# The first two feed-forward blocks of a streaming encoder layer, quarter by quarter while the rows are being turned

## The chip, the cores and the metric

One Trainium2 chip, one of its cores. The kernel is one launch on that core: one layer of a streaming encoder. The metric is the device time of one execution in microseconds (us), lower is better. The kernel before has a median of 2502.78 us over 3 runs (2499.66 to 2502.88).

Engines are named as in the profile: PE is the matrix engine (PEld its weight loads), DVE the vector engine, ACT the scalar engine, POOL the general engine, SP the engine that issues most transfers. Each engine works through its own instructions in the order in which they stand in the built program; an instruction that waits holds up all behind it on its engine.

## The reference, cut to what matters

The layer is a feed-forward block, a mixer (attention and a recurrent branch, merged by gates) and a second feed-forward block, on T = 1072 frames (16 meta tokens, 1024 prompt frames, 32 frames of running streams) of D = 1024 channels.

```python
D_MODEL = 1024
SEQ = 1024
DEC_SEQ = 32
N_META = 16
D_FF = 2816
EPS = 1e-6

def rmsnorm(x, g):
    xf = x.astype(jnp.float32)
    y = xf * lax.rsqrt(jnp.mean(xf * xf, axis=-1, keepdims=True) + EPS)
    return (y * g.astype(jnp.float32)).astype(x.dtype)

def half_ffn(x, g, w_gate, w_up, w_down):
    h = rmsnorm(x, g)
    return x + 0.5 * ((jax.nn.silu(h @ w_gate) * (h @ w_up)) @ w_down)
...
def reference(...):
    ...
    x = half_ffn(x, ffn1_norm[l], ffn1_w_gate[l], ffn1_w_up[l], ffn1_w_down[l])
    h = rmsnorm(x, mix_norm[l])
    ... (mixer)
    x = half_ffn(x, ffn2_norm[l], ffn2_w_gate[l], ffn2_w_up[l], ffn2_w_down[l])
    ... (final norm)
```

The change is at the start of the first feed-forward (the norm and the first columns of `h @ w_gate`, `h @ w_up`) and at the same place of the second.

## The kernel before, in words

**Products in three parts.** Each float32 operand is split in a high part (`xh`, `whi`; a copy that rounds, on ACT) and a low part (`xl`, `wlo`; the difference, on DVE). A product is `whi*xh + whi*xl + wlo*xh`. `product()` makes one such product for four 128-row slices of the channels (half of the 1024, called `kh` 0 or 1) and one quarter of the frames (268 columns): 12 matmuls of 128x268 into one PSUM bank, all on line L103 of the profile. The split of a tile is `split()` (L219 on ACT, L220 on DVE), that of a weight tile `weights()` (L202 on ACT, L203 on DVE).

**Quarters.** The frames are cut into four quarters of 268, called q0 to q3; `b` is q // 2 and `th` is q % 2. `B[kh, th, b]` is the split pair of half the channels of a quarter.

**The first feed-forward** (`Seven`, tiles of pool `f1`). The 2816 columns are 22 blocks of 128. Blocks 0 and 1 are multiplied plainly by `plain(c)`: for each quarter gate with kh 0 and 1, then up with kh 0 and 1, so 192 matmuls a block and 384 for the two. Blocks 2 to 21 go in pairs ("units", `rest()`) by a scheme of seven half products for two by two; it needs sums of the halves, `T1` to `T4` for each b, made by `sums(b)` (L819, L826, L828, L829, each a 128x1072 DVE operation, and four splits). The gated results are split into a stage (tiles `R`, `st`) and sent to DRAM (`mid_dram`) by POOL.

**What comes before block 0.** The frames are loaded as rows: for each quarter two tiles `xt` of 128 rows, and one tile `odds` that holds the last 12 rows of all four quarters. The row tiles of q0 and q1 lie in slots with the tag `g`, those of q2 in `raw2`, those of q3 in the two slots with the tag `S`. For each quarter `scales` makes the reciprocal root mean square per row (squares summed on ACT, L761; seven small operations on DVE and POOL, L764 to L770, of which POOL's power is L766), `spread` puts it on a diagonal (POOL, L778 and L781), multiplies ones by it on PE and copies the result to `R` (ACT, L783): the scale of each frame in all partitions. `columns(q)` turns the rows: for each of 8 channel slices three PE transposes (two row tiles and the odd rows, all on L106; below, one channel slice of a quarter is called a column), an ACT copy of the turned rows to a tile `s` (L809, sent to DRAM as the residual), a DVE operation that multiplies them by gain and scale (L810), and after each four slices the split into `xh`, `xl`.

**What sets the order.** The tile scheduler that builds the program orders each engine by its own estimates of readiness, unless `PE.on` is set: then PE's instructions keep the order in which they are written. In the first feed-forward it is off before the change. A tile is taken from a tag with so many slots; the first instruction that writes a new tile in a slot waits until the last reader of the tile that was there is done.

**The second feed-forward** begins with `ff.plain(0, ...)`, in written order, behind `out_block`, the last product of the mixer. There the norm of the last 288 frames is still under way while q0 is multiplied: `finish_one()` holds what is left of it (`scale_rows`, L264 and L119 on ACT with the functions Ln and Exp, L267 to L270 on DVE, then `kept`'s multiplications L1661 and splits). `silu` is L119 as well, with another table of functions on ACT; a change of table is an ACT_TABLE_LOAD (L113).

## Time and profile before

| What | Time or share |
|---|---|
| Median of 3 runs (lowest to highest) | 2502.78 us (2499.66 to 2502.88) |
| The profiled execution | 2499.49 us, its span 2497.4 us |
| PE busy in the span | 2403.0 us, 96% |
| DVE, ACT, POOL busy in the span | 67%, 41%, 10% |
| First product of block 0 | 36.70 us |
| First product of unit 1, after blocks 0 and 1 | 97.17 us |
| First product of the second feed-forward | 1764.56 us |

The times in the rows of the profile are us from the start of the span. A row of the timeline is: start, duration, engine, line, operation, written tile, read tiles, shapes, how many in a row, and in square brackets the idle time of the engine just before it with what ended it. In the chain of waits a row is: start, length, engine, tile and line. Durations of neighbours overlap on all engines (a matmul of 268 columns is shown with 0.28 us and the next begins 0.12 us after it), so sums go by starts, or by the chain of waits, which has only what is not covered.

### The profile page before, as it was taken

The numbers are of one execution on the slowest core, as the hardware profiler recorded it, in microseconds if no ns is written. First come the engines' busy times: TensorE is split into PE (matmuls) and PEld (weight loads), VectorE is DVE, ScalarE is ACT, GpSimd is POOL, SyncE is SP. The second block draws the span as 40 slices with busy tenths as digits, with TensorE's granted clock in tenths as the row PEclk, the third lists the DMA queues.
The fourth block names the chain that finished last, engine by engine and source line by source line (L and its number), as shares of the span: only waits on it lengthen the run. The fifth ranks groups of instructions, "written<-read, shape, count | busy, mean of one in ns | idle before, by whom it ended". The sixth has DMA issues, their size and how long they took to land.

```text
span 2497.4 us, 47900 instructions
## 1 busy us (share of the span) xinstructions
PE 2403.0 (96%) x19500; PEld 2299.1 (92%) x19500; DVE 1669.2 (67%) x3144; ACT 1021.3 (41%) x2129; POOL 257.2 (10%) x461
## 2 busy tenths in 40 slices
PE   6999999989998999999999999999799999989997
PEld 5999999979998999999788888999799999989997
DVE  4767676758865377774666665556966767666876
ACT  6444444542225243332545544323544444443223
POOL 1001010100003011221000000111011111110000
PEclk9999999999999999999999999999899999999999
DMA  7334343477651211111211122522244444467761
GB/s 197 105 122 166 122 166 122 164 292 280 245 210 62 60 44 56 48 49 53 57 44 49 44 64 67 190 86 98 75 136 153 143 147 147 143 266 267 274 235 71
DMA packets 270371, 331.93 MB, mean 133 GB/s; under 512 B 41078, under 2 KB 228726, under 8 KB 264518
## 3 DMA queue, kind: packets, MB, share of 16 engines
q1 hardware_dynamic: 247942, 244.96, 29.7%
q0 software_dynamic: 22208, 83.91, 8.9%
q8 instruction: 153, 2.51, 0.4%
q14 instruction: 68, 0.56, 0.1%
HBM read 213.93 MB, written 114.89 MB: 132 GB/s over the span
## 4 chain that ended last, share of the span: by engine, by line
PE 54%; issue 29%; DVE 6%; DMA 4%; POOL 4%; ACT 3%; POOLq 0%; SPq 0%; DVEq 0%; ACTq 0%
PE ps_mm L103 20%; PE ps_z L103 11%; PE pu L103 6%; PE ps_o L103 5%; PE pv L103 4%; PE pf L103 4%; POOL mid_dram L353 3%; DMA mid_dram<-st 2%; PE ps_tr L103 2%; PE ps_tr L106 2%; PE ps_z L106 1%; DMA u_xl<-mid_dram 1%; DVE wlo L203 1%; PE ps_mm L106 0%; DVE acc L1661 0%
## 5 line engine op out<-in xcount | busy, mean ns | idle before, releaser
L103 PE MATMUL ps_mm<-xh,whi 128*128 128x384 f32 (+2 forms) x952 | 316.8, 333 | 0.5 <-DVE raw L1455 0.5
L103 PE MATMUL ps_mm<-xh,wlo 128*128 128x384 f32 (+2 forms) x952 | 310.4, 326 | 0.0
L103 PE MATMUL ps_mm<-xl,whi 128*128 128x384 f32 (+2 forms) x952 | 309.9, 326 | 0.0
L219 ACT ACTIVATE whi<-S 128x1024 fp32r<-128x1024 f32 x122 | 129.2, 1059 | 310.7 <-PE ps_z L103 138.0
L353 POOL DMA_DIRECT2D mid_dram<-st x148 | 102.7, 702 | 872.7 <-DVE st L220 854.9
L103 PEld LDWEIGHTS ps_mm<-xh,whi 128*128 128x128 f32 x952 | 179.3, 188 | 9.0 <-issue 5.0
L103 PEld LDWEIGHTS ps_mm<-xl,whi 128*128 128x128 f32 x952 | 179.4, 188 | 1.1
L103 PEld LDWEIGHTS ps_mm<-xh,wlo 128*128 128x128 f32 x952 | 179.5, 189 | 0.3
L220 DVE TENSOR_TENSOR wlo<-S,whi 128x1024 fp32r<-128x1024 f32 x122 | 149.2, 1223 | 37.8 <-ACT whi L219 35.2
L220 DVE TENSOR_TENSOR st<-g,st 128x536 fp32r<-128x536 f32 (+1 forms) x148 | 103.5, 709 | 100.2 <-ACT st L219 100.1
L1247 DVE TENSOR_TENSOR_SCAN left<-left,oneb 128x512 f32<-128x512 f32 (+6 forms) x112 | 107.4, 959 | 54.8 <-ACT left L119 54.2
L202 ACT ACTIVATE whi<-raw 128x1024 fp32r<-128x1024 f32 x67 | 70.5, 1056 | 172.6 <-PE ps_mm L103 135.8
L219 ACT ACTIVATE st<-g 128x536 fp32r<-128x536 f32 (+1 forms) x148 | 93.5, 643 | 96.6 <-DMA mid_dram<-st 82.4
L220 DVE TENSOR_TENSOR wlo<-raw,whi 128x1024 fp32r<-128x1024 f32 x80 | 76.6, 958 | 72.6 <-ACT whi L219 70.9
L103 PE MATMUL ps_z<-acc1s,whi 128*128 128x268 f32 (+1 forms) x480 | 106.3, 285 | 0.0
L103 PE MATMUL ps_z<-xh1s,whi 128*128 128x268 f32 (+1 forms) x360 | 102.8, 286 | 0.0
L103 PE MATMUL ps_z<-xl1s,whi 128*128 128x268 f32 (+1 forms) x360 | 102.6, 285 | 0.0
L103 PE MATMUL ps_z<-xh1s,wlo 128*128 128x268 f32 (+1 forms) x360 | 102.6, 285 | 0.0
L103 PE MATMUL ps_z<-xh2s,whi 128*128 128x268 f32 (+1 forms) x352 | 100.5, 286 | 2.2 <-ACT s L458 2.2
L103 PE MATMUL ps_z<-xl2s,whi 128*128 128x268 f32 (+1 forms) x352 | 100.4, 285 | 0.0
L103 PE MATMUL ps_z<-xh2s,wlo 128*128 128x268 f32 (+1 forms) x352 | 100.3, 285 | 0.0
L203 DVE TENSOR_TENSOR wlo<-raw,whi 128x1024 fp32r<-128x1024 f32 x67 | 82.8, 1240 | 23.3 <-ACT whi L202 23.1
(719 smaller groups left out, 7636.2 us busy)
## 6 DMA issues: line engine op xcount, KB each, us to landing
mid_dram<-st POOLq DMA_DIRECT2D x74, 536.0 KB, 4.2
mid_dram<-st POOLq DMA_DIRECT2D x74, 528.0 KB, 3.9
raw<-in_ffn_w_gate_dram SPq DMA_DIRECT2D x44, 512.0 KB, 3.8
raw<-in_ffn_w_up_dram SPq DMA_DIRECT2D x44, 512.0 KB, 3.9
raw<-in_w_in_dram SPq DMA_DIRECT2D x44, 512.0 KB, 3.7
raw<-in_ffn_w_down_dram SPq DMA_DIRECT2D x40, 512.0 KB, 5.3
u_xl<-mid_dram SPq DMA_DIRECT2D x8, 1608.0 KB, 6.5
u_xh<-mid_dram SPq DMA_DIRECT2D x8, 1608.0 KB, 10.4
```

Source lines behind the costliest of these rows:

```text
L103: return self.queue(nc.tensor.matmul(*args, **more))
L106: return self.queue(nc.tensor.transpose(*args, **more))
L202: A.activation(hi, raw, AF.Copy)
L203: V.tensor_tensor(lo, raw, hi.bitcast(F32), op=ALU.subtract)
L219: A.activation(dst_h, src, AF.Copy)
L220: V.tensor_tensor(dst_l, src, dst_h.bitcast(F32), op=ALU.subtract)
L353: nc.gpsimd.dma_start(self.mids[i, :, :, NAMES.index(name)], st.bitcast(F32))
L1247: V.tensor_tensor_scan(rev(st[:rows]), rev(st[:rows]), one, 1.0 if carry is None else carry[:rows], op0=ALU.mult, op1=ALU.mult)
```

## The change

- `plain` takes several blocks. Blocks 0 and 1 of the first feed-forward are multiplied together: for each quarter, kh 0 of gate 0, up 0, gate 1, up 1 (steps j = 0 to 3), then kh 1 of the same (j = 4 to 7); 12 matmuls a step. PE's order is as written (`PE.on`). Behind single steps other work is emitted: after j = 0 of q1, q2, q3 the columns of that quarter's kh 1; after j = 3 `spread` of the next quarter, and the scales and the diagonal of the quarter after it (now on POOL); after j = 5 the columns of the next quarter's kh 0; `sums(0)` after j = 6 of q2, `sums(1)` after j = 1 of q3.
- The loads on SP stand in another order: rows of q0, odd rows, gate and up weights of block 0, rows of q1 and q2, then the weights of block 1 among the rows of q3. The four weight tiles use the two slots of `raw`.
- q0 is turned by a function of its own (`first_columns`): rows of the first row tile first, diagonal on DVE, splits in halves of two channel slices (128x536), the eighth slice behind the second step.
- One Square of 1024 elements in place of two of 512. `odds` is cleared on DVE in place of POOL.
- `sums` makes all four differences first, then the splits; T1, T2, T3 get other homes, T4 of b = 0 is split at once.
- Products of a tile of zeros (128x512, bf16) are put on PE: 18 at the start, 6 ahead of the first ones-by-diagonal, 5 ahead of the first product.
- In the second feed-forward q0 of block 0 now goes gate kh 0, up kh 0, gate kh 1, up kh 1, with both weights requested ahead, and `finish_one()` is called after the silu of the quarter.
- Two small operations (`causalb`, `lmax`) are tied behind a product, so that they don't come early.

The diff, without the parts that only pass results on:

```diff
-        def plain(self, c, before=lambda q: None, after=lambda q: None):
+        def plain(self, cs, step=lambda q, j: None, tags=(None,) * 2):
...
             for q in range(4):
-                before(q)
                 b, th = divmod(q, 2)
-                pss = []
-                for wh, wl in (gw, uw):
-                    ps = bank(rotate=True)
-                    for kh in range(2):
-                        ks = slice(kh * 512, (kh + 1) * 512)
-                        product(ps, (wh[:, ks], wl[:, ks]), self.B[kh, th, b], kh == 0)
-                    pss.append(ps)
-                after(q)
-                silu(where(g, th, b), pss[0][:, :qw])
-                V.tensor_tensor(where(g, th, b), pss[1][:, :qw], where(g, th, b), op=ALU.mult)
+                pss = [bank(tag, tag is None) for tag in tags]
+                for kh in range(2):
+                    ks = slice(kh * 512, (kh + 1) * 512)
+                    for j, (wh, wl) in enumerate(x for c in cs for x in ws[c]):
+                        product(pss[j], (wh[:, ks], wl[:, ks]), self.B[kh, th, b], kh == 0)
+                        to = where(gs[cs[j // 2]], th, b)
+                        if kh and j % 2 == 0:
+                            silu(to, pss[j][:, :qw])
+                        elif kh:
+                            V.tensor_tensor(to, pss[j][:, :qw], to, op=ALU.mult)
+                        step(q, kh * len(pss) + j)
...
+        row_tiles(0)
+        for x in range(4):
+            load(odds, 32 * x, x * QW + 2 * P, ODD)
+        raw_weights(0)
+        row_tiles(1)
+        row_tiles(2)
+        raw_weights(1)
+        row_tiles(3)
...
+        def warm(n, ps):
+            for _ in range(n):
+                PE.matmul(ps, busy[:, :P], busy[:, P:P + 512], start=True, stop=True)
...
         def sums(b):
 
             v11, v12, v21, v22 = (value(*x, b) for x in ((0, 0), (0, 1), (1, 0), (1, 1)))
-            t1, t2 = f32s("S"), f32s("S")
+            t1, t2, t4, t3 = f32s("S"), f32s("S"), f32s("s"), f32s("s")
             V.tensor_tensor(t1, v12, v11, op=ALU.subtract)
...
             V.tensor_tensor(t2, v22, t1, op=ALU.subtract)
+            V.tensor_tensor(t4, v21, t2, op=ALU.subtract)
             V.tensor_tensor(t3, v22, v12, op=ALU.subtract)
...
+        def step(q, j):
+            if (q, j) == (0, 1):
+                first_rest()
+            if q < 3:
+                if j == 3:
+                    spread(q + 1)
+                    if q < 2:
+                        diagonal(q + 2, scales(rows[2 * q + 4:2 * q + 6], G, latest[0]), odd, G)
+                elif j == 5:
+                    columns(q + 1, 0)
+            if q and j == 0:
+                columns(q, 1)
+            if (q, j) in ((2, 6), (3, 1)):
+                sums(q - 2)
+
+        ff.plain((0, 1), step, ("mm", "mm", "tr", "o"))
...
-        ff.plain(0, after=lambda q: finish_one())
+        ff.ahead[0] = [gate0[0], ff.block(ffn2_w_up, 0)]
+        ff.plain((0,), lambda q, j: j == 3 and finish_one())
```

Three places where the order of instructions moves:

DVE around the turning of q3. `S` and `s` are the tiles of `sums`, `xl2s` is the low part of q3, `acc0s`, `acc1s` and `xe` hold the scaled frames. Before:

```order
L810 SCALAR_TENSOR_TENSOR acc1s<-ps_z,gains,R 128x268
L819 TENSOR_TENSOR S<-acc0s 128x1072
L220 TENSOR_TENSOR xl2s<-acc1s,xh2s 128x1072
L826 TENSOR_TENSOR S<-acc0s,S 128x1072
L390 TENSOR_TENSOR g<-ps_z,g 128x268
L220 TENSOR_TENSOR acc2s<-S,acc2s 128x1072
L829 TENSOR_TENSOR s<-xe_126,S 128x1072
L828 TENSOR_TENSOR S<-acc0s 128x1072
```

And in the change (L846 is the old L810, L229 the old L220, L903 to L906 are the differences of `sums`):

```order
L846 SCALAR_TENSOR_TENSOR acc1s<-ps_z,gains,R 128x268 x4
L229 TENSOR_TENSOR xl2s<-acc1s,xh2s 128x1072
L397 TENSOR_TENSOR g<-ps_o,g 128x268
L903 TENSOR_TENSOR S<-acc0s 128x1072
L904 TENSOR_TENSOR S<-acc0s,S 128x1072
L905 TENSOR_TENSOR s<-xe_137,S 128x1072
L906 TENSOR_TENSOR s<-acc0s 128x1072
L229 TENSOR_TENSOR xe_768<-S,xe_767 128x1072
L229 TENSOR_TENSOR xl1s<-s,xh1s 128x1072
L229 TENSOR_TENSOR acc0s<-S,acc0s 128x1072
L229 TENSOR_TENSOR xe_769<-s,acc0s 128x1072
```

Directly behind these eight stand `L846 ... acc1s` x4, the last four channel slices of q3, then L903 of `sums(1)` and the last `xl2s`. So the four differences and four splits of `sums(0)` stood behind the last scaling of q3, and now stand ahead of its second half.

ACT at the second feed-forward: `ms` and `ys` are the norm of the last 288 frames, `g` the silu of a quarter. Before:

```order
L264 ACTIVATE ms<-ps_z,epsb 128x288
L119 ACTIVATE ys<-ms 128x288
L119 ACTIVATE ys<-ys 128x288
L113 ACT_TABLE_LOAD
L119 ACTIVATE g<-ps_z 128x264
L119 ACTIVATE g<-ps_tr 128x264
L219 ACTIVATE acc0s<-S 128x1056
L219 ACTIVATE xh1s<-acc_17872 128x4x24 x2
```

And in the change:

```order
L119 ACTIVATE g<-ps_z 128x264
L273 ACTIVATE ms<-ps_z,epsb 128x288
L119 ACT_TABLE_LOAD
L119 ACTIVATE ys<-ms 128x288
L228 ACTIVATE acc0s<-S 128x1056
L119 ACT_TABLE_LOAD
L119 ACTIVATE ys<-ys 128x288
L119 ACT_TABLE_LOAD
L119 ACTIVATE g<-ps_mm 128x264
L228 ACTIVATE xh1s<-acc_17873 128x4x24 x2
```

The silu of q0 went ahead of Ln and Exp (the two `ys`), and a table load stands ahead of each of Ln, Exp and the next silu; the table of silu itself is loaded some rows earlier (L113). A split (`acc0s`) stands between Ln and Exp.

SP at the start. Before:

```order
L734 DMA odds<-in_x_sample_dram 12x1024
L734 DMA xt<-in_x_prompt_dram 128x1024 x5
L734 DMA xt<-in_x_prompt_dram 108x1024
L734 DMA xt<-in_x_sample_dram 20x1024
L192 DMA raw<-in_ffn_w_gate_dram 128x8x128
L192 DMA raw<-in_ffn_w_up_dram 128x8x128
```

And in the change:

```order
L742 DMA odds<-in_x_sample_dram 12x1024
L762 DMA raw<-in_ffn_w_gate_dram 128x8x128
L762 DMA raw<-in_ffn_w_up_dram 128x8x128
L742 DMA xt<-in_x_prompt_dram 128x1024 x4
L762 DMA raw<-in_ffn_w_gate_dram 128x8x128
L742 DMA xt<-in_x_prompt_dram 128x1024
L762 DMA raw<-in_ffn_w_up_dram 128x8x128
L742 DMA xt<-in_x_prompt_dram 108x1024
```

The weights of block 0 passed six row tiles; those of block 1, which stood behind all rows and behind two transfers of the residual, stand among the rows.

More of the change, by code (lines that the diff above doesn't have):

```diff
@@ L183, in tile_encoder_step, with planned, weights @@
     big = Wide
-    def weights(parts, own=None):
-        raw = wp.tile([P, D], F32, tag="raw", name="raw", bufs=2)
+    def planned(made, last):
+        tc.add_manual_dep(made.ins, last.ins.name, order, reason="order")
+    def weights(parts, own=None, raw=None, behind=None, later=None):
         n = 0
+        if raw is None:
+            raw = wp.tile([P, D], F32, tag="raw", name="raw", bufs=2)
         for src, k in parts:
@@ L201, in weights @@
             hi, lo = own()
-        A.activation(hi, raw, AF.Copy)
-        V.tensor_tensor(lo, raw, hi.bitcast(F32), op=ALU.subtract)
+        made = A.activation(hi, raw, AF.Copy)
+        if behind is not None:
+            planned(made, behind)
+        made = V.tensor_tensor(lo, raw, hi.bitcast(F32), op=ALU.subtract)
+        if later is not None:
+            planned(made, later)
         return hi, lo
@@ L838, in sums @@
-            split(*X["T2", b], t2)
-            split(*X["T3", b], t3)
-            return t4
-        def columns_ahead(q):
-            if q == 0:
-                r = scales(rows[0:2] + [odds])
-                found.append(r[2])
-                spread(0, r[:2], found[0])
-                columns(0)
-            if q < 3:
-                spread(q + 1, scales(rows[2 * q + 2:2 * q + 4]), found[0])
-                columns(q + 1)
-        found = []
-        ff.plain(0, columns_ahead)
-        t4s = [sums(b) for b in range(2)]
@@ L855, in tile_encoder_step @@
-        ff.plain(1)
+                X["T1", b] = extra(2, F32R), extra(0, F32R)
+                X["T2", b] = free[:, 0], free[:, 1]
+                X["T3", b] = free[:, 2], extra(3, F32R)
+            else:
+                X["T1", b] = free[:, 0], free[:, 1]
+                X["T2", b] = free[:, 2], extra(1, F32R)
+            split(*X["T1", b], t1)
+            split(*X["T2", b], t2)
+            if b == 1:
+                free = slots("acc", 2, F32R)
+                X["T3", b] = free[:, 0], free[:, 1]
@@ new lines, in sums @@
+            split(*X["T3", b], t3)
+            X["T4", b] = B[0, 1, b]
+            X["B11", b], X["B21", b], X["B22", b] = B[0, 0, b], B[1, 0, b], B[1, 1, b]
+            if b == 0:
+                split(*X["T4", b], t4)
+            else:
+                ff.t4 = t4
+        PE.on = True
+        r = scales([rows[0], odds, rows[1]], V)
+        odd = r[1]
+        wsq = [weights([], None, raws[0][0], latest[0], diagonal(0, [r[0], r[2]], odd, V))]
+        first_rest = first_columns()
+        diagonal(1, scales(rows[2:4], G, latest[0]), odd, G)
@@ new lines, in tile_encoder_step @@
+        up1 = slots("acc", 2, F32R)
+        own = lambda: [up1[:, x].rearrange("p k t -> p (k t)")[:, :D] for x in range(2)]
+        ff.ahead.update({0: wsq, 1: [weights([], own if x else None, raw, latest[0])
+                                     for x, raw in enumerate(raws[1])]})
+        def step(q, j):
+            if (q, j) == (0, 1):
+                first_rest()
+            if q < 3:
+                if j == 3:
[8 more added lines that the diff above has]
+                sums(q - 2)
@@ L856, in tile_encoder_step @@
+        ff.plain((0, 1), step, ("mm", "mm", "tr", "o"))
+        PE.on, PE.last = False, None
+        split(*X["T4", 1], ff.t4)
         constants()
-        for b in range(2):
-            X["T4", b] = B[0, 1, b]
-            split(*X["T4", b], t4s[b])
-            X["B11", b], X["B21", b], X["B22", b] = B[0, 0, b], B[1, 0, b], B[1, 1, b]
         ff.rest()
```

165 lines of the change are left out of this document (102 added, 63 removed).

## The prediction

> **What bounds the kernel now.** I first read the page's shares (PE 96% busy), then a table of windows, since the change touches only the first 120 us and some 30 us at 1764. Its columns: from, to, length; busy time of PE, PEld, DVE, ACT, POOL; granted PE clock; DMA share; GB/s.
>
> ```profile
> 0.00:36.70 36.70, 15.96 (x60) 10.65 (x61) 13.18 (x46) 24.42 (x60) 9.79 (x19) 1.00 0.63 183
> 36.70:64.50 27.80, 27.80 (x180) 24.44 (x181) 18.93 (x35) 14.00 (x26) 1.51 (x3) 1.00 0.88 220
> 64.50:97.20 32.70, 32.70 (x267) 32.70 (x266) 27.78 (x31) 13.72 (x18) 1.42 (x2) 1.00 0.20 66
> 112.00:122.00 10.00, 7.79 (x49) 7.42 (x48) 5.50 (x9) 4.78 (x10) 1.38 (x2) 0.83 0.56 187
> ```
>
> Up to 36.70 PE has no product and is idle for more than half of the time; from there to 97.2, through blocks 0 and 1, it never waits. So two things count: when the first product starts, and whether PE is still fed without a gap. DVE is busy for 46.7 of those 60.5 us, the engine nearest to its limit. PE's waits in the head:
>
> ```profile
> PE ps_z L106 <- DMA xt<-in_x_prompt_dram: 8.2, 2, 7.0
> PE ps_mm L103 <- POOL t_ys L778: 5.7, 1, 5.7
> PE ps_z L103 <- POOL t_ys L778: 3.8, 1, 3.8
> PE ps_mm L103 <- DVE acc0s L810: 2.8, 1, 2.8
> ```
>
> The chain of waits gives prices (start, length, what):
>
> ```profile
> 36.70 5.72 PE ps_mm L103 x24
> 42.42 3.05 PE ps_z L103 x24
> 45.48 0.76 PE ps_tr L103 x6
> 46.24 0.53 PE ps_z L106 x3
> ...
> 70.13 1.19 DVE s L829
> 71.32 1.19 DVE S L828
> 72.54 1.11 ACT acc0s L219
> ...
> 74.13 1.18 DVE acc0s L220
> ```
>
> Twenty-four products take 3.05 us at full clock (0.124 each after rounding over the stretch) and 5.72 at half; one spread 0.76, one column 0.53; a 1072-wide difference or split costs DVE 1.18, and ACT 1.1.
>
> **The change part by part.**
>
> *An earlier first product.*
>
> ```profile
> 9.79 0.63 ACT L761 ACTIVATE t_ms<-xt 128x512 bf16<-128x512 f32 x1 [1.39 <-DMA xt<-in_x_prompt_dram]
> 14.75 0.16 DVE L764 TENSOR_TENSOR ss<-ss 128x3 f32<-128x3 f32 x1 [11.36 <-ACT t_ms L761]
> 16.80 0.16 DVE L770 TENSOR_TENSOR ss<-ss 128x3 f32<-128x3 f32 x1
> 17.74 1.92 PE L103 MATMUL ps_mm<-t_ys,cst 128*128 128x128 f32 x6 [5.70 <-POOL t_ys L778]
> 20.94 0.50 DVE L810 SCALAR_TENSOR_TENSOR acc0s<-ps_mm,gains,R 128x268 f32<-128x268 f32 x1 [0.33 <-ACT s L809]
> 21.36 0.49 DVE L810 SCALAR_TENSOR_TENSOR acc0s<-ps_z,gains,R 128x268 f32<-128x268 f32 x1
> ```
>
> The second row tile lands at 9.79. In the change its square is the last of three: 1.2 us (under two halves of 0.63) gives 11.0. The small chain now takes 14.75 to 16.96 = 2.2; less the addition, 2.0: 13.0. The diagonal on DVE has no row; its three instructions lie between the small operations' 0.16 and the 0.50 of a 268-wide row, 0.5 to 1.5 in all; I take 0.7, nearest to the small rows as 128 elements are few: 13.7. Ones by diagonal 0.76 to 1.92, the copy to R 0.4, two scalings of 0.41 (20.94 to 21.36), half a split 0.55: first product at 17 (16 to 19.5), a **gain of 19.7 us** at that point. The zeros run while PE waits for rows and squares, so 0; the last five can cost up to 1.1, if they stand in the way at half clock.
>
> *PE's work behind it.* Now 16 of 32 columns and two spreads lie before 36.70. In the change only seven columns and one spread do: nine columns (4.8) and one spread (0.76) move into the fed stretch. It then holds 384 products (47.6), 25 columns (13.2), three spreads (2.3): **63.2 us** at full clock. The first 24 products or so are at half clock as now: +2.7 (0 if the zeros had raised it for good).
>
> *Weights.*
>
> ```profile
> L192 SPq DMA_DIRECT2D raw<-in_ffn_w_gate_dram x2: 373/386/400, 11.4 to 35.1; - x2
> DMA to landing us min/median/max: 4.1/7.1/10.4
> 33.88 2.36 DVE L203 TENSOR_TENSOR wlo<-raw,whi 128x1024 fp32r<-128x1024 f32 x2
> ```
>
> Block 0's weights pass six row tiles and are there in time. Block 1's cannot be requested before `raw` is free: gate 1 behind gate 0's `wlo` (about 15.3, right after the diagonal), up 1 behind up 0's (about 20, behind four scalings and two splits). Behind the waiting request on SP stand the rows of q3, which nobody needs before 75. Landing 4.1 to 10.4 later, split in 2.2: gate 1 is ready at 21.6 to 28, up 1 at 26 to 32. PE wants them at about 21 and 24. I take **6 us** of gaps in q0 (3 to 10).
>
> *Each turn to a new quarter.* The next quarter's kh 0 columns end with j = 5; PE then has j = 6 and 7 as cover, 3.0 us. ACT's split stands behind the silu that waits for j = 6 (1.5 us after the columns), then 0.4 for the silu, 1.1 for the high part, 1.2 for the low: 4.2. Gap 1.2, three times: **3.6**.
>
> *The second half of q3, where I expect the loss.* `sums(0)` is emitted before the last columns, and its first two results are written in the two slots `S`, which hold q3's rows: DVE's first difference waits until PE has turned the last column. Only then: four differences, four splits (8 x 1.18 = 9.4), four scalings (1.6), the high split on ACT (1.1), the low one on DVE (1.2): 13.3 us. Behind the waiting difference are queued the scalings that PE's next step needs. PE's cover is j = 1 to 3, 4.5 us. **Gap 8.9**. Were the slots free, DVE could begin about 3.2 us earlier; 5.7 would stay. In the order of before the same 9.4 us lay behind the last scaling, with PE busy on products (64.50 to 97.20 above).
>
> What a gap costs beside itself:
>
> ```profile
> 116.11 0.39 PE L103 MATMUL ps_z<-xh2s,whi 128*128 128x268 f32 x1 [2.17 <-ACT s L458]
> 117.78 0.43 PE L103 MATMUL ps_tr<-xh1s,whi 128*128 128x268 f32 x1
> 121.09 0.29 PE L103 MATMUL ps_z<-xh2s,whi 128*128 128x268 f32 x1
> ```
>
> After a gap of 2.17 us the products ran at half clock from 117.58 to 120.9 (spacing 0.22), 1.5 us lost. A gap of 8.9 costs this too: **+1.7**, at most 3.
>
> Sum for unit 1's first product: 17 + 63.2 + 2.7 + 6 + 3.6 + 8.9 + 1.7 = 103.1, against 97.17: **+5.9** (bounds 94 and 110).
>
> *Unit 1.* The gap of 2.17 and its half clock, 3.7 us, came from ACT waiting on stages that were still being sent. With blocks 0 and 1 ending together and ACT idle in q3, the stages go out elsewhere; but `sums(1)` and unit 1's weight sums now follow right behind the gap and can be late themselves. **-2** (-3.7 to +1.5).
>
> *The second feed-forward.*
>
> ```profile
> 1764.56 0.28 PE L103 MATMUL ps_z<-xh0s,whi 128*128 128x264 f32 x1
> 1774.97 0.59 PE L103 MATMUL ps_mm<-xh0s,wlo 128*128 128x264 f32 x1 [7.11 <-DVE wlo L203]
> 1779.94 1.13 PE L103 MATMUL ps_z<-t_ga,cst 128*128 128x288 f32 x4
> 1781.11 0.50 ACT L264 ACTIVATE ms<-ps_z,epsb 128x288 f32<-128x288 f32 x1 [2.17 <-PE ps_z L103]
> 1782.12 0.44 ACT L119 ACTIVATE ys<-ys 128x288 f32<-128x288 f32 x1
> 1782.59 1.28 ACT L113 ACT_TABLE_LOAD   x1
> 1782.60 0.46 DVE L267 TENSOR_TENSOR ms<-ms,ys 128x288 f32<-128x288 f32 x1
> 1783.88 0.39 ACT L119 ACTIVATE g<-ps_z 128x264 f32<-128x264 f32 x1
> 1785.54 0.45 DVE L270 TENSOR_TENSOR R<-ys,ms 128x288 f32<-128x288 f32 x1
> 1785.65 1.09 ACT L219 ACTIVATE acc0s<-S 128x1056 fp32r<-128x1056 f32 x1 [1.10 <-DVE S L1680]
> 1787.58 0.28 PE L103 MATMUL ps_o<-xl1s,whi 128*128 128x264 f32 x1
> 1787.87 0.26 DVE L220 TENSOR_TENSOR xl1s<-acc,xh1s 128x96 fp32r<-128x96 f32 x1
> ```
>
> PE waits 7.11 us for up's low part, with all 24 gate products done under earlier work. In the new order gate's kh 1 stands behind up's kh 0, which waits for the same `wlo`: 12 products (1.46) come out from under it, and everything behind is 1.46 later. The norm of the last 288 frames gets two table loads (2 x 1.28) and a split (1.09) into its chain, 3.65. DVE's four operations behind Exp took 3.4 us (1782.60 to 1785.99), some 1.4 of it for other work in between that will now be done earlier; q2's operand, which today is there 0.3 us around PE's arrival, is then late by 2.2 to 3.6, less some 15 products of block 1 that the order puts ahead of q2 (1.8): 0.4 to 1.8. **+2.5** (+1 to +5). [...]
>
> Sum: 5.9 - 2 + 2.5 = +6.4. The profiled execution took 2499.49 (2.1 outside its span), so 2505.9; it is the fastest of the runs shown, 3.3 under the median, and I carry the difference to the median: 2509.2, rounded to **2509**.
>
> **The rivals.**
>
> *Not slower (0.13).* One mechanism: the feed of q0. If the weights of block 1 land within 4 us of being requested, and the clock is full from the first product (the zeros count), the 8.7 us of gaps and half clock in q0 go: unit 1 starts at 94.4 (-2.8), and the total is -2.3: 2500. For: 4.1 us is the shortest landing shown. Against: the longest is 10.4, and rows are in transfer at that time. It decides when gate 1's `whi` is ready before 21.
>
> *The gap of q3 is not there (0.13).* If the scalings of q3 were not held (`sums(0)` served before the last columns), unit 1 starts at 92.5, -4.7; the total is -4.2: 2498.6. For: DVE is only busy 85% of 64.50 to 97.20. Against: the slots `S` and the order of DVE.
>
> *No change to speak of (0.16).* The gap is there, PE's head gains as planned, feed gaps of 3, half clock short: unit 1 at 98 to 100, unit 1's own gap gone, +0 to +2: about 2504.
>
> *Worse (0.13).* Block 1's weights land 10 us after the request and half clock stays through q0 (another 24 to 48 products at 0.1 more): unit 1 at 109, total +13: 2516.
>
> The forecast itself has 0.45, 2508 to 2513. A measurement of this kernel can tell about 0.2% (5 us) from no change; below 2497.8 is faster, above 2507.8 slower. Faster 0.12 (half of the second rival, some of the first), same 0.30, slower 0.58. The range 2498 to 2517 leaves out the best of the rivals of the other sign and the tail of the worst.
>
> **What would show it.** Right: first product at 16 to 20; gaps of some us on PE between 20 and 32 with block 1's `whi`, `wlo` or `acc2s` as releasers; one wait of 7 to 9 us on ACT's `xh2s` between 85 and 98, with L903 to L906 and four L229 on DVE under it and the granted clock under 1 behind it; unit 1 at 100 to 106; two more table loads and a PE wait near 9 us at 1766 to 1775. Wrong: a first product after 22; no wait on `xh2s`, or one under 3; unit 1 before 95.

## The result, and the profile after

| | Before | Changed |
|---|---|---|
| Median (lowest to highest), 4 runs each | 2502.83 us (2499.66 to 2505.11) | 2517.80 us (2513.11 to 2520.83) |
| Ratio of the medians, 95% interval | | 1.0060 [1.0047, 1.0073] |
| The profiled execution and its span | 2499.49, 2497.4 | 2520.83, 2518.8 |

The change makes the kernel 15.0 us slower (11.8 to 18.3 by the interval). The forecast was slower by 6.4, 2509, with a range that ended at 2517: the sign was right, the size was not, and the median lies 0.8 us beyond the range.

The windows of the changed kernel's head, with the columns of the prediction's table:

```profile
17.00:36.70 19.70, 17.11 (x88) 14.01 (x88) 9.04 (x16) 11.71 (x22) 5.07 (x11) 0.75 0.77 186
...
84.00:92.00 8.00, 4.35 (x36) 4.13 (x34) 7.88 (x7) 5.20 (x8) 0.00 (x0) 0.99 0.01 2
92.00:103.00 11.00, 6.11 (x29) 5.80 (x30) 9.88 (x13) 4.85 (x8) 0.74 (x1) 0.54 0.27 100
103.00:122.00 19.00, 18.07 (x145) 17.64 (x144) 18.94 (x27) 11.04 (x20) 1.37 (x2) 1.00 0.34 114
```

PE works in q0 (first row) with few gaps but a quarter of the clock missing. From 84 to 103 it works for just over half of the time, while DVE is never idle for long; and it is DVE that stays full, 18.94 of 19.00 us, when PE is busy again. PE's waits in the same kernel up to 170 us (what PE was to do, who ended the wait, us, times, longest):

```profile
PE ps_mm L103 <- ACT xh2s L228: 7.8, 1, 7.8
...
PE ps_mm L103 <- DVE xl1s L229: 1.8, 2, 0.9
PE ps_mm L103 <- DVE xl2s L229: 1.6, 2, 0.9
...
PE ps_tr L103 <- DVE wlo L210: 0.7, 1, 0.7
...
```

The waits for rows and diagonals of 7 and 5.7 us are gone, and one of 7.8 us stands in their place. The timeline of PE in the changed kernel, at its first product, at that wait, and at the first product of unit 1:

```profile
17.08 2.32 PE L103 MATMUL ps_mm<-busy 128*128 128x512 bf16 x5 [1.02 <-DVE acc0s L846]
18.83 0.78 PE L103 MATMUL ps_mm<-xh0s,whi 128*128 128x268 f32 x1
...
88.06 0.28 PE L103 MATMUL ps_o<-xh2s,acc2s 128*128 128x268 f32 x1
96.17 0.59 PE L103 MATMUL ps_mm<-xh2s,whi 128*128 128x268 f32 x1 [7.83 <-ACT xh2s L228]
97.48 0.59 PE L103 MATMUL ps_mm<-xl2s,whi 128*128 128x268 f32 x1 [0.72 <-DVE xl2s L229]
...
105.41 0.29 PE L103 MATMUL ps_mm<-xh0s,whi 128*128 128x268 f32 x1
```

And what DVE does meanwhile:

```profile
83.49 1.27 DVE L903 TENSOR_TENSOR S<-acc0s 128x1072 f32<-128x1072 f32 x1 [3.06 <-PE ps_z L106]
84.86 1.28 DVE L904 TENSOR_TENSOR S<-acc0s,S 128x1072 f32<-128x1072 f32 x1
...
92.10 1.27 DVE L229 TENSOR_TENSOR xe<-s,acc0s 128x1072 fp32r<-128x1072 f32 x1
93.29 1.70 DVE L846 SCALAR_TENSOR_TENSOR acc1s<-ps_z,gains,R 128x268 f32<-128x268 f32 x4
94.91 1.26 DVE L903 TENSOR_TENSOR S<-acc1s 128x1072 f32<-128x1072 f32 x1
96.15 1.27 DVE L229 TENSOR_TENSOR xl2s<-acc1s,xh2s 128x1072 fp32r<-128x1072 f32 x1
```

DVE waits 3.06 us until PE has turned q3's last column (the slots `S`), then does the eight operations of `sums(0)`, and only at 93.29 the four scalings that PE waits for, though PE had turned the first of their columns at 82.1. Unit 1's first product is at 105.41, 8.2 us later than in the kernel before.

That leaves 7 us to find. I numbered PE's matrix instructions, zeros left out, and compared the times at which both kernels reach the same number. The difference grows at four places, two of which lie where no line of the change is: in the mixer, and in a stretch that starts 150 us before the end. Single executions differ by some us elsewhere too, and the profiled pair are the two extremes (the change's is the slowest of its four, that of before is faster than its four in the table). So the table takes means over the profiles of the runs told of below, one execution of each kernel:

| Stretch of PE's instructions | With the cause | Without it | Difference |
|---|---|---|---|
| 0 to 1000: the first feed-forward's start, as changed or as before | 166.9 us (4 profiles, 165.9 to 168.2) | 160.3 (4, 158.6 to 162.8) | +6.6 |
| 11,800 to 13,000: the mixer, in the change's order or in that of before | 172.5 (5, 171.9 to 172.9) | 168.9 (8, 167.4 to 169.5) | +3.6 |
| 13,500 to 14,500: the second feed-forward's start, as changed or as before | 156.5 (6, 156.2 to 156.9) | 154.0 (9, 153.6 to 155.1) | +2.5 |
| 18,400 to 19,400: near the end, with or without the zeros | 128.4 (9, 127.2 to 129.0) | 126.0 (6, 125.8 to 126.4) | +2.4 |

The sum is 15.1.

**The mixer.** At about 1558 us narrow products (`aT` with `vc` or `vs`, 32 columns) alternate with wide ones (`xh`, `xl`, 384 columns). The timeline of PE before:

```profile
1559.25 0.86 PE L103 MATMUL ps_o<-aT,vc 16*64 16x32 f32 x10
1560.04 0.45 PE L103 MATMUL ps_mm<-xh,whi 128*128 128x384 f32 x1
1560.32 0.34 PE L103 MATMUL ps_mm<-xl,whi 128*128 128x384 f32 x1
1560.50 0.34 PE L103 MATMUL ps_mm<-xh,wlo 128*128 128x384 f32 x1
1560.68 0.51 PE L103 MATMUL ps_mm<-xh,whi 128*128 128x384 f32 x2
1561.12 0.30 PE L103 MATMUL ps_o<-aT,vs 32*64 32x32 f32 x2
```

And at the same place of the changed kernel, with a row from a few us later:

```profile
1570.10 0.86 PE L103 MATMUL ps_o<-aT,vc 16*64 16x32 f32 x10
1570.89 0.57 PE L103 MATMUL ps_mm<-xh,whi 128*128 128x288 f32 x2
1571.39 0.30 PE L103 MATMUL ps_o<-aT,vs 32*64 32x32 f32 x2
...
1577.99 1.39 PE L103 MATMUL ps_o<-aT,vc 16*64 16x32 f32 x10
```

Five wide products stand between these narrow groups before, two in the change, one of 288 and one of 384 columns (the row names only the first one's shape); between all groups of that stage it is 14 and 11. A little later ten narrow products take 1.39 us where they took 0.86. The windows of that stage, 20 us from the first narrow group on, before:

```profile
1558.20:1578.20 20.00, 20.00 (x172) 18.41 (x172) 11.80 (x29) 4.66 (x10) 0.00 (x0) 1.00 0.53 178
```

and in the change:

```profile
1569.00:1589.00 20.00, 20.00 (x134) 17.66 (x134) 10.28 (x28) 4.65 (x10) 0.00 (x0) 0.66 0.31 98
```

PE has no gap in either, but in the change the granted clock is 0.66 over the window: it is half for 13.7 of the 20 us. In four other kernels with this order it is half for 13.7 or 17.1 us. All half-clock stretches in these traces are multiples of 3.41 us (3.41 to 13.65 in the change), but for the last one of each trace, which the end cuts off. Elsewhere half clock stood behind waits of PE: 0.50 from 117.6 to 120.9 us in the kernel before, behind 2.17 us. What it stands behind here isn't shown. The profile has PE busy for 20.00 of 20.00 us, without a wait; but it models where a matmul ends. Ten narrow products start 0.079 us apart (1559.25 to 1560.04), and at the pace of the wide ones (384 columns in 0.18) 32 columns would take 0.015. By that estimate PE stands idle for most of a narrow group; no run shows whether that lowers the clock.

In the other two orders that were run (that of before, and one of e10 and e11) the clock is full among the narrow groups in all ten traces. Eight of the ten have 3.4 us of half clock later, some 27 us behind the first narrow group, where PE waits for `ga`, as in e2:

```profile
1585.24 0.45 PE L103 MATMUL ps_z<-xh,whi 128*128 128x384 f32 x1 [1.76 <-DVE ga L1631]
```

Half clock followed waits of 1.76 us and more there, and none followed those of 1.67 (the kernel before) and 1.53 us (e13). In the change's order PE comes later and waits 0.3 us at most. So the stage is spared a wait and the half clock behind it while it runs 13.7 to 17.1 us at half clock, and 3.6 us of loss are left.

Why is the order another one, in code that was not touched? `bank(rotate=True)` hands out PSUM banks in a cycle of eight. The columns, spreads and products of blocks 0 and 1 drew 52 of them before (32 + 4 + 16), the change names its banks there and draws none. So everything behind draws from a place shifted by 52 mod 8 = 4, banks come free at other moments, and the scheduler, whose order is free there (`PE.on` is off), puts other products between the narrow ones. In the mixer PE's order in the change is, row for row, that of the kernel before with its counter moved by 4 (e6, below).

**Near the end.** PE's wait near the end in the kernel before:

```profile
PE pv L103 <- DMA u_xl<-mid_dram: 0.7, 1, 0.7
```

The same wait in the change, and the queues' share from the issue of those transfers to their use (packets, MB, share of 16 engines):

```profile
PE pv L103 <- DMA u_xl<-mid_dram: 2.4, 1, 2.4
...
q1 hardware_dynamic: 914, 4.14, 91.7%
q8 instruction: 1, 0.02, 0.5%
```

In the kernel before no packet of q8 lies in this stretch. `u_xl` comes in two transfers of 1584 KB, issued as far ahead of PE's arrival as before (the first 9.4 us); but one fetch of PE's own program, 16 KB, now falls among them, 7 us behind the second issue. Before it falls 12 us behind, after PE has gone on. PE's gap of 2.4 us has 3.4 us of half clock behind it, some 3 us in all (129.0 against 125.8). Behind the fetch's shift are the 29 products of zeros, 58 instructions more on PE (a product and a weight load each); the queue's 2.51 MB in 153 packets make 16 KB each, and 64 bytes for each of the 39,058 products and weight loads of PE, by which I take the queue for PE's. Over the 15 traces fetch and wait go together: with the fetch at 7 us PE goes on 11.4 to 11.8 us behind the first issue (the nine kernels with zeros), without it 10.1 to 10.3 (five of the six others; the sixth is e13, below). No run moves a fetch alone, so that the fetch delays the transfer is argued from this, not shown.

### The profile page after: what moved, and what is told of

The parts are those of the page before. It is cut to its first block, busy times and chain, and to the rows that moved or that the text cites. A ratio compares the mean times of both kernels' runs of the same rounds, so it can differ in the third digit from the quotient of the medians.

```text
span 2518.8 us, 47945 instructions
## 1 busy us (share of the span) xinstructions
PE 2426.2 (96%) x19529; PEld 2313.0 (92%) x19529; DVE 1669.3 (66%) x3131; ACT 1024.0 (41%) x2113; POOL 260.0 (10%) x472
## 3 DMA queue, kind: packets, MB, share of 16 engines
q8 instruction: 153, 2.51, 0.4%
## 4 chain that ended last, share of the span: by engine, by line
PE 55%; issue 29%; DVE 6%; POOL 4%; DMA 3%; ACT 3%; POOLq 0%; DVEq 0%; SPq 0%; ACTq 0%
PE ps_mm L103 20%; PE ps_z L103 11%; PE pu L103 6%; PE ps_o L103 5%; PE pv L103 4%; PE pf L103 4%; POOL mid_dram L362 4%; DMA mid_dram<-st 2%; PE ps_tr L103 2%; PE ps_tr L106 1%; PE ps_z L106 1%; DMA u_xl<-mid_dram 1%; DVE wlo L210 0%; DVE acc L1759 0%; ACT whi L207 0%
## 5 line engine op out<-in xcount | busy, mean ns | idle before, releaser
L229 DVE TENSOR_TENSOR wlo<-S,whi 128x1024 fp32r<-128x1024 f32 x122 | 149.1, 1223 | 33.3 <-ACT whi L228 30.6
L229 DVE TENSOR_TENSOR st<-g,st 128x536 fp32r<-128x536 f32 (+1 forms) x148 | 103.4, 709 | 87.9 <-ACT st L228 87.7
L207 ACT ACTIVATE whi<-raw 128x1024 fp32r<-128x1024 f32 x66 | 69.5, 1056 | 172.6 <-PE ps_mm L103 138.5
L229 DVE TENSOR_TENSOR wlo<-raw,whi 128x1024 fp32r<-128x1024 f32 x80 | 76.6, 957 | 72.2 <-ACT whi L228 70.4
L228 ACT ACTIVATE whi<-raw 128x1024 fp32r<-128x1024 f32 x80 | 67.6, 845 | 70.7 <-PE ps_z L103 64.2
L103 PE MATMUL ps_z<-xh1s,whi 128*128 128x264 f32 (+1 forms) x336 | 95.9, 285 | 0.0
L103 PE MATMUL ps_z<-xl1s,whi 128*128 128x264 f32 (+1 forms) x336 | 95.8, 285 | 0.0
L103 PE MATMUL ps_z<-xh1s,wlo 128*128 128x264 f32 (+1 forms) x336 | 95.7, 285 | 0.0
L103 PE MATMUL ps_z<-xl2s,whi 128*128 128x264 f32 (+1 forms) x336 | 95.7, 285 | 0.0
L103 PE MATMUL ps_z<-xh2s,whi 128*128 128x264 f32 (+1 forms) x336 | 95.7, 285 | 0.0
## 6 DMA issues: line engine op xcount, KB each, us to landing
u_xh<-mid_dram SPq DMA_DIRECT2D x8, 1608.0 KB, 11.8
```

The costliest lines, as they stand in the source:

```text
L103: return self.queue(nc.tensor.matmul(*args, **more))
L207: made = A.activation(hi, raw, AF.Copy)
L228: return (A.activation(dst_h, src, AF.Copy), V.tensor_tensor(dst_l, src, dst_h.bitcast(F32), op=ALU.subtract))
L229: V.tensor_tensor(dst_l, src, dst_h.bitcast(F32), op=ALU.subtract))
```

## The experiments

**e1: the first feed-forward's part alone.** The second is written as before, its block 1 too.

```diff
-        ff.ahead[0] = [gate0[0], ff.block(ffn2_w_up, 0)]
-        ff.plain((0,), lambda q, j: j == 3 and finish_one())
+        ff.ahead[0] = gate0[0]
+        ff.plain_one(0, after=lambda q: finish_one())
```

> The change's part in the first feed-forward alone; the second feed-forward as before (gate kh 0, kh 1, then up; norm finished before the silu). Theory A (the losses lie where they were named: feed of q0, the gap of 7.8 us before q3's second half and the half clock behind it, the order of the second feed-forward; the rest of the +15 is half clock that falls elsewhere by chance): +5 on the median of before, 2508 (2506 to 2511), first product of unit 1 at 102 to 104, two table loads less. Theory B (the other 7 us come from the first part too, through the order that it leaves on PE in the mixer): +10 to +13, 2513 to 2516. Theory C (the second feed-forward makes most of it): under +3.

Measured: 2514.25 us, ratio 1.0050 [1.0037, 1.0062], +12.5. The stretch in the mixer was at half clock for 17.1 us, instructions 0 to 1000 took 165.9. Most of the loss comes from this part, and some of it arises far behind it.

**e2: the second feed-forward's part alone**, on the kernel before (the same two lines the other way round).

> The change's part in the second feed-forward alone, on the kernel before. Theory A and B: +2, 2505 (2503.5 to 2507): PE's wait for up's low part grows from 7.1 to about 8.5 us, and a second wait of at most 2 us stands before q2's products. Theory C: +8 or more.

Measured: 2504.29, 1.0009 [1.0000, 1.0019], +2.3; its stretch took 156.6 in place of 154.1. The mixer has 3.4 us of half clock, behind the wait for `ga`.

**e3: the sums later.** `sums(0)` behind the last columns of q3, so that DVE serves the scalings first.

```diff
-            if (q, j) in ((2, 6), (3, 1)):
-                sums(q - 2)
+            if (q, j) in ((3, 1), (3, 3)):
+                sums(0 if j == 1 else 1)
```

> The change with the sums of b = 0 emitted behind the turning of q3's second half (after j = 1 of q3, those of b = 1 after j = 3). If the wait of 7.8 us on q3's second half comes from DVE's queue and the row slots, it falls under 2 us and unit 1 starts at 91 to 94 in place of 102.7. But DVE then has 19 us of sums and 6 us of weights' work ahead of unit 1's third product, which PE reaches 16 us later: a new wait of 5 to 9 us there, and the time is within 3 us of the change. Rival: DVE's work is not what counts, the wait was the rows' transfer or a slot: then the wait on q3 stays, or no new one appears and the whole gains 10 us.

Measured: 2513.87, 1.0048 [1.0035, 1.0061]. The wait on `xh2s` is gone and PE's instruction 500 comes at 92.2 (104.9 in the change), but unit 1 waits in its place:

```profile
PE ps_mm L103 <- DVE wlo L229: 4.5, 1, 4.5
PE ps_mm L103 <- DVE g L397: 2.6, 1, 2.6
```

By instruction 1000 it is at 164.6: of the 12.7 us, 3.6 are left. (The expectations of e3, e4 and e8 put unit 1's first product in the change at 102.7; by its row it is 105.41.)

**e4: the sums earlier.** `sums(0)` in pieces from q1 on, its results in the slots of `g`, which the rows of q1 have left.

```diff
+        first_sums = {(1, 2): differences, (1, 4): fourth, (2, 2): first_two, (2, 6): third_high, (3, 2): third_low}
...
-            if (q, j) in ((2, 6), (3, 1)):
-                sums(q - 2)
+            if (q, j) in first_sums:
+                first_sums[q, j]()
+            if (q, j) == (3, 1):
+                sums(1)
```

> The change with the sums of b = 0 taken early, in four pieces between j = 2 of q1 and j = 2 of q3, with their first two differences in slots of g in place of those of q3's rows. Theory A: no wait over 2 us before q3's second half, unit 1's first product at 92 to 95 (102.7 in the change), no wait over 3 us in unit 1, and 8 to 11 us less than the change: 2507 to 2510. Rival (DVE is full in blocks 0 and 1, so its work comes back as gaps at the turns of q1 and q2): unit 1 at 97 or later, under 5 us gained.

Measured: 2510.88, 1.0043 [1.0029, 1.0057]. Instruction 500 at 92.6, instruction 1000 at 159.8, 0.5 ahead of the mean of before: the gap is taken away, and the early start still gains next to nothing. The window of e4 around unit 1's start shows why:

```profile
84.00:105.00 21.00, 17.29 (x128) 17.05 (x128) 21.00 (x25) 11.51 (x17) 1.42 (x2) 0.92 0.25 87
```

DVE is busy for 21.00 of 21.00 us (15.67 in the kernel before). `sums(1)` and the first unit's weight sums stand in one row there, however early PE comes.

**e5: the change with the bank counter put back**, and **e6: the kernel before with the counter moved**, nothing else, so that e6 has the banks of the change and e5 those of before.

```diff
+        rot[0] += 4
```

> The change, and behind blocks 0 and 1 the counter that hands out PSUM banks in rotation moved on by 4. The kernel before drew 52 banks in rotation up to there (4 in step with the cycle of 8), the change draws none; with the 4 added, PE's order in the mixer is the order of before again, where in the change three of five 384-wide products left a run of short products (aT by vc, 64x32). Theory B (this order makes the granted clock fall to half for 13 to 17 us around 1570 to 1600): half clock there at most 3.4 us, and 4 to 5.5 us less than the change: about 2513. Theory A (half clock there is chance): it is there as before, within 1.5 us of the change's 2517.8 and of the 2514.3 + 1.7 of its parts.

> The kernel before, with nothing but the bank counter moved on by 4 behind blocks 0 and 1, so that PE's order in the mixer is that of the change. Theory B: +4 to +5.5 on the median of before, 2507 to 2508, with 13 to 17 us of half clock between 1555 and 1590. Theory A: 2502.6 as before, within 1.5.

Measured: e5 2512.76, 1.0054 [1.0040, 1.0067]; half clock in the mixer 3.4 us, its stretch 169.5 in place of 171.9. e6 2504.05, 1.0008 [0.9998, 1.0018]; half clock there 17.1 us, 172.9. One line that computes nothing moves the clock of a stage 1460 us later, both ways. The price was put too high: +2.0 for e6, with an interval from -0.5 to +4.5, so that the time alone doesn't tell it from nothing; the traces do (172.9 against 167.4 to 169.5). The window of e6, from its first narrow group:

```profile
1557.00:1577.00 20.00, 20.00 (x128) 17.67 (x128) 10.11 (x27) 4.65 (x10) 0.00 (x0) 0.60 0.31 97
```

**e7: early sums (e4), the second feed-forward as before (e1), the counter put back (e5)**: all that was known by then to cost, taken out.

> The three repairs together: first feed-forward of the change with the early sums, second feed-forward as before, bank counter in step. Theory A and B: unit 1 at 92 to 95 (97.2 before), the gain of 2.5 to 3 us behind unit 1 kept to the end: 2499 to 2501, against 2502.6 before. Rival (the clock falls in some other stage, whatever is repaired): 2503 or more.

Measured: 2501.88, 1.0007 [0.9997, 1.0017]: no difference to before. PE reaches instruction 500 at 92.7 and 1000 at 160.9, where the mean of before is 160.3. Its waits in unit 1 are small, but with the 6.8 us of half clock that lie around them (3.4 lost) they take back what the early start won:

```profile
PE ps_o L103 <- DVE g L419: 1.5, 1, 1.5
PE ps_tr L103 <- ACT g L119: 1.1, 1, 1.1
```

**e8: as e5, without the 29 products of zeros.**

```diff
...
-            warm(before, ps)
...
-            warm(18, pss[-1])
...
-            warm(5, bank("mm"))
+            bank("mm")
...
```

> The change with the bank counter in step and without the 29 products of zeros; nothing else. If the zeros raise the clock for the first products: q0's products and transposes run at half clock for longer, unit 1's first product 1.5 to 4 us later than with them (102.7). If the feed of q0 covers what they gain: within 1 us.

Measured: 2511.73, 1.0039 [1.0026, 1.0052], not slower than e5. Instruction 500 comes at 102.9 (104.2 in e5), so the zeros bring nothing at the start, where the expectation looked for their effect; but the stretch near the end took 125.9 in place of 128.9.

**e9: as e7, with two of the differences of `sums(1)` on POOL.**

```diff
-            V.tensor_tensor(t4, v21, t2, op=ALU.subtract)
-            V.tensor_tensor(t3, v22, v12, op=ALU.subtract)
+            G.tensor_tensor(t4, v21, t2, op=ALU.subtract)
+            G.tensor_tensor(t3, v22, v12, op=ALU.subtract)
```

> The changed first feed-forward with the sums of q0 and q1 made early in four pieces, the mixer's order of the kernel before (the bank counter put forward by 4), the second feed-forward as before, and the two differences t3 and t4 of the second pair of quarters moved from DVE to POOL. Theory (at unit 1's head DVE's own queue is the bound, 81.7 to 105 us without a gap): DVE has 2.4 us less there, the two waits of PE in unit 1 (1.5 on g, 1.1 on the turned rows' bank) shrink to under 1 in all, and the time comes to about 2499.5, 2 us under the run without the move. Rival (POOL takes longer for a 128x1072 difference than DVE has room for, and PE then waits for t3 or t4): a new wait of 2 to 5 us in unit 1, and 2503 to 2507. Half clock in the mixer stage: 3.4 us, as in the order of before.

Measured: 2504.44, 1.0005 [0.9996, 1.0014]: no difference to before or to e7. It is the rival's time, but not by its way. The waits did not shrink; PE waits 3.8 us for `g`. The two operations on POOL:

```profile
87.39 2.89 POOL L927 TENSOR_TENSOR s<-xe,S 128x1072 f32<-128x1072 f32 x1 [30.88 <-DVE S L926]
90.24 3.45 POOL L928 TENSOR_TENSOR s<-acc1s 128x1072 f32<-128x1072 f32 x1
```

and DVE in the same run:

```profile
88.76 2.60 DVE L229 TENSOR_TENSOR wlo<-raw,whi 128x1024 fp32r<-128x1024 f32 x1 [0.88 <-ACT whi L228]
91.28 0.42 DVE L419 TENSOR_TENSOR g<-ps_mm,g 128x268 f32<-128x268 f32 x1
91.63 3.19 DVE L229 TENSOR_TENSOR xl2s<-s,xh2s 128x1072 fp32r<-128x1072 f32 x1
94.85 1.27 DVE L229 TENSOR_TENSOR acc1s<-S,acc1s 128x1072 fp32r<-128x1072 f32 x1
```

Splits that take 1.21 (`wlo`, in e7) and 1.27 us without POOL take 2.60 and 3.19 beside it, and each ends 1.1 us behind the end of an operation of POOL (90.28 to 91.36, 93.69 to 94.82). The product with `ps_mm`, one of whose operands lies in PSUM, keeps its 0.42 (0.43 in the change, at 80.00). The 1.4 and 1.9 us lost are about the rest of POOL's instruction (1.5 and 2.1), as if each split had waited for its end; what held them, and why the product was not held, isn't shown. The two differences took 2.4 us off DVE, and its splits lost 3.3 beside them.

**e10: the kernel before, counter moved by 1** (17 wide products between the narrow groups), and **e11: as e9, counter moved by 5** in place of 4 (17 too, the same order).

```diff
+        rot[0] += 1
```

> The kernel before, with the bank counter put forward by 1 instead of 4 at the end of the first feed-forward: nothing but the banks behind it changes, and with them the order in the mixer stage at about 1560 us, where 17 products then stand between two groups of 64x32 products (14 in the kernel before, 9 with the counter put forward by 4). Theory (the more wide products stand between the groups of narrow ones, the less of that stage runs at half clock): half clock there 0 to 3.4 us, 2500 to 2503. Rival (any other order than that of before costs the same, because a scheduler's order that was measured and kept is lost): half clock of 13 to 17 us, 2504 to 2507.

> As the run with t3 and t4 on POOL, but the counter put forward by 5 (17 products between the groups in the mixer stage, as in the kernel before with its counter put forward by 1). Theory: as that run, within 1 us, and under it by up to 2 if the half clock of 3.4 us in the mixer stage goes: 2497.5 to 2500. Rival (POOL's differences come late): the same 2 to 5 us of wait in unit 1, 2503 to 2507.

Measured: e10 2501.70, 1.0002 [0.9992, 1.0012], 3.4 us of half clock in the mixer; e11 2502.12, 0.9999 [0.9989, 1.0009]. e11 lies between its theory's time and the rival's. Another order than that of before is not slower as such: of the three orders tried (11, 14 and 17 wide products; the expectation counts 9 in place of 11, without the two of the first gap) only the one with 11 has the long half clock, and 17 bring nothing over 14.

**e12: the kernel before, with the 29 products of zeros at PE's start**, and **e13: e7 without its zeros** (the lines that e8 removes).

```diff
+        for n in (8, 7, 7, 7):
+            ps = bank("z")
+            for _ in range(n):
+                PE.matmul(ps, busy[:, :P], busy[:, P:P + 512], start=True, stop=True)
```

> The kernel before, with 29 products of zeros put at PE's very start, where PE has nothing to do until rows arrive at 9 us; the order of everything else is that of before but for 8 of 18084 rows of PE. Theory (the zeros' 58 instructions shift the points at which PE's program is fetched, and one such fetch of 16 KB then falls into the last big transfer of staged rows, u_xl, 7 us behind its issue instead of 12): the fetch at 7, PE's wait for u_xl near the end 2.0 to 2.4 us instead of 0.7, half clock of 3.4 us behind it, 2 to 3 us more at the end than in the kernel before: 2504 to 2505. Rival (the fetch has no part in it; the wait was late for another reason in the kernels with the changed first feed-forward): 0.7 us of wait, same time as before, 2501 to 2503.

> The run with the changed first feed-forward, early sums, the second feed-forward as before and the mixer's old order (2501.88 us), without its 29 products of zeros; the order of all else is the same row for row. Theory (the zeros cost 2 to 3 us at the end of the program by way of the fetch, and bring nothing at its start): wait for u_xl 0.7 us, no half clock behind it, 2499 to 2500, 2 to 3 us under the kernel before. Rival: the fetch has no part in it, 2501 to 2503.

Measured: e12 2503.52, 1.0012 [1.0003, 1.0021], +3.0 (0.8 to 5.3). The fetch lies at 7 us, and near the end PE waits as in the change, with 3.4 us of half clock behind it:

```profile
PE pv L103 <- DMA u_xl<-mid_dram: 2.0, 1, 2.0
```

Its stretch near the end took 128.7 (125.8 before). So the zeros, on a kernel that is otherwise the same, cost some 3 us 2400 us later. e13 is only half a confirmation. In its trace the fetch of q8 lies at 13 us, the wait is 1.3, no half clock follows and the stretch takes 126.4 in place of 128.8. (That the wait is not 0.7 goes with a fetch of 8 KB in another instruction queue, q14, 7.6 us behind the second issue.) Nor does every such wait cost its half clock: in e9 and e11, with the zeros, PE waits 2.1 and 2.0 us, none follows, and the stretch takes 127.3 and 127.2. But the time of e13, 2504.08, 1.0006 [0.9998, 1.0015], is not under that of e7 (1.0007); its profiled execution, at 2498.08, was the fastest of its twelve. What the other executions lose instead isn't shown. The zeros' price so rests on the traces and on e12.

Put together, the four differences of the table are set against the time of each kernel, by the parts that it carries. In e3, e4, e7 and e13 the first term is their own instruction 1000 less the 160.3 of before. The differences come from profiles of the same kernels, so the table shows whether they suffice; it is no forecast.

| Run | Parts | Sum, us | Measured, us [95%] |
|---|---|---|---|
| the change | all four | 15.1 | 15.0 [11.8, 18.3] |
| e1 | 6.6 + 3.6 + 2.4 | 12.6 | 12.5 [9.3, 15.5] |
| e3 | 4.3 + 3.6 + 2.5 + 2.4 | 12.8 | 12.0 [8.8, 15.3] |
| e4 | -0.5 + 3.6 + 2.5 + 2.4 | 8.0 | 10.8 [7.3, 14.3] |
| e5 | 6.6 + 2.5 + 2.4 | 11.5 | 13.5 [10.0, 16.8] |
| e8 | 6.6 + 2.5 | 9.1 | 9.8 [6.5, 13.0] |
| e6 | 3.6 | 3.6 | 2.0 [-0.5, 4.5] |
| e2 | 2.5 | 2.5 | 2.3 [0.0, 4.8] |
| e12 | 2.4 | 2.4 | 3.0 [0.8, 5.3] |
| e7 | 0.6 + 2.4 | 3.0 | 1.8 [-0.8, 4.3] |
| e13 | -0.9 | -0.9 | 1.5 [-0.5, 3.8] |

All sums but that of e13 lie in the intervals.

## Why the prediction was right in sign and short in size

**The first feed-forward, term by term.** The terms measured between the rows at 18.83 and 105.41 of the changed kernel, where the second is what the others leave:

| Term | Forecast | Measured |
|---|---|---|
| First product | 17 | 18.83 |
| Products, columns, spreads at full clock | 63.2 | 66.7 |
| Half clock | 4.4 | 6.1 |
| Gaps in q0, for weights | 6 | 2.4 |
| Gaps at three turns | 3.6 | 2.8 |
| Gap in the second half of q3 | 8.9 | 8.55 |
| Unit 1's first product | 103.1 | 105.4 |

*First product*: inside its bounds of 16 to 19.5. The five zeros ahead of it ran at half clock (0.51 from 16.8 to 20.2 us), but they were not what it waited for: without them, in e8, it came at 18.95. *Full clock*: the 384 products were priced at 0.124 each from a stretch in which they ran without a break. Cut into steps by spreads and waits they cost 0.133 to 0.136, by whether a column is put at the 0.53 of the forecast or at its 0.49 here. The chain of waits of the change shows it at the turn to the second half of q3:

```profile
70.56 3.16 PE ps_mm L103 x24
73.72 1.96 PE ps_z L106 x12
75.68 1.69 PE ps_tr L103 x12
...
80.14 1.62 PE ps_mm L103 x11
```

Twenty-four products behind a spread take 3.16 where 2.98 was reckoned, and eleven behind a wait 1.62 where it was 1.36. Twelve behind four columns take 1.69 for 1.49, but the columns give most of that back (1.96 for 2.12). The chain of before has 3.16 and 3.17 for such 24 as well, behind columns, so a part of this could have been read. *Gaps in q0*: up 1's second half was ready at 29.1, inside the 26 to 32 forecast, but PE came later itself, since its first product was 1.8 us later and it ran at half clock up to 20.2 and again from 27.0 to 33.9 us (0.51), and so met shorter gaps. *Second half of q3*: the step that carried the forecast. It came out at the place, with the operations and the releaser named, 7.83 and 0.72 against 8.9, and the half clock behind it.

**Unit 1, -2.** In the profiled pair the stretch from instruction 500 to 1000 did become 2.8 us shorter (66.1 to 63.2). But the wait of 2.17 us in one piece and the half clock behind it, which the term counted as a gain, belong to that one execution of the kernel before: in e2, e6 and e10 PE waits 1.2 to 2.0 us in all for the same tile, no half clock follows, and the stretch took 63.4 to 64.4. Against these three the gain is 0.7. The step failed in taking a property of one execution for one of the kernel. By means over four profiles of each kind, the changed kernels are 7.8 us behind at instruction 500 (5.9 forecast) and win 1.2 from there to 1000 (2 forecast): a loss of 6.6 us, where 5.9 - 2 = 3.9 was forecast.

**The second feed-forward, +2.5.** Measured: 2.5. PE's wait there was forecast near 9:

```profile
PE ps_o L103 <- DVE wlo L210: 8.4, 1, 8.4
```

A second wait before q2's products, forecast at 0.4 to 1.8, took 0.5 on `xh1s` here and 1.0 on `g` in e2.

ACT's rows show the two table loads and the split in the norm's chain:

```profile
1798.19 1.28 ACT L119 ACT_TABLE_LOAD   x1
1799.49 0.45 ACT L119 ACTIVATE ys<-ms 128x288 f32<-128x288 f32 x1
1799.84 1.07 ACT L228 ACTIVATE acc0s<-S 128x1056 fp32r<-128x1056 f32 x1
1800.93 1.28 ACT L119 ACT_TABLE_LOAD   x1
...
1802.69 1.28 ACT L119 ACT_TABLE_LOAD   x1
```

Ln starts 0.02 us behind the end of the first load, so that the load took 1.28 us of the chain and little beside.

**What the sum left out.** It ended with the second feed-forward's head, and took all between and behind as unmoved. This is the step that failed, with 3.6 us in the mixer and 2.4 near the end that the sum put at nothing: 6.0 of the 8.6 us by which it was short. The other 2.7 are those of the first feed-forward, 6.6 against 3.9. Both could be asked of the code: the part on the order compared only places near the change, while the scheduler's freedom and the bank counter reach all the way; and "the zeros run while PE waits, so 0" priced their time, not their instructions. That the stage in the mixer would answer with half clock could not be read from the trace of before, which shows no fall there.

**The rivals.** "Not slower" rested on weights landing within 4 us. Up 1 took 4.85 from request to landing, gate 1's `whi` was ready at 24.4 and not before 21, and the zeros didn't spare the half clock in q0: the granted clock was 0.75 from 17.0 to 36.7. "The gap of q3 is not there" was made true by e3 and e4. Unit 1's start came out as it named (instruction 500 at 92.2 and 92.6, for 92.5), but by instruction 1000 only 0.5 us of gain on before was left in the better one, not 4.2: the price was wrong since DVE has no room behind it. "Worse" (2516) came nearest to the time, by a mechanism that did not occur. "No change to speak of" held neither in the head nor in the time.

**What stays open.** Why the granted clock falls among narrow products, and how many wide ones prevent it, is bounded only by the three orders tried; whether PE is idle inside the narrow groups isn't shown. That a fetch delays the transfer, and the zeros' price in whole times, rest on what is said of e12 and e13. The two tied operations, `causalb` and `lmax`, were not run by themselves. Between 470 and 910 us and between 2160 and 2350 us the stretches of single profiles differ by up to 5 us with the half clock that they happen to have, in kernels of both kinds; no part of the change could be told from that.

## What to carry to other kernels

An early start on one engine is worth only what the next bound lets through: count the work of the second-busiest engine behind the place, here DVE's sums in front of unit 1 (busy for 21.00 of 21.00 us in e4), before pricing the gain. An edit moves more than its lines where a counter deals out banks or a scheduler orders freely (in e6 one line brought 17.1 us of half clock 1460 us later), so compare the built order to the very end of the program, and pin or restore the counter when testing an edit. Filler instructions can have a price by the program's length as well as by their time (+3.0 us in e12, 0.8 to 5.3), and a wait seen in one execution is no term of a sum until a second one shows it.

## What the runs showed of the hardware

- The granted clock fell to half for 13.7 to 17.1 us in a stage in which the profile shows no gap of PE, when 11 wide products stood between groups of products of 32 columns (five traces); with 14 or 17 it stayed full there (ten traces).
- With a fetch of 16 KB of PE's program inside two transfers of 1584 KB, PE went on 1.3 (e12) to 1.7 us (the change) later than before, though the fetch is 0.5% of the DMA engines' time in that stretch.
- A difference of 128x1072 on POOL took 2.9 to 3.5 us beside DVE (1.27 on DVE), and two splits on DVE beside it took 2.60 and 3.19 us in place of 1.21 and 1.27, each ending 1.1 us behind an operation of POOL (e9).
